# Two-layer trunk (RG-LRU, then forgetting attention): per-head work moved between query groups, output operands made in head 14, the first MLP product's pools swapped, small copies and sums on VectorE

## The chip, the cores and the metric

The kernel runs on one core of a Trainium2 chip. The metric is the device time of one execution in microseconds (us). The kernel before took 2306.42 us, the median of three runs (2304.84 to 2311.81).

## The reference

One sequence of 1024 positions, width 1024, goes through two layers in float32. Each layer adds a mixer and then an MLP to the residual stream.

```python
for layer in range(2):
    h = rms_norm(x, mix_norm[layer])
    x = x + (rglru_mixer(h) if layer == 0 else fox_mixer(h))
    x = x + square(relu(rms_norm(x, mlp_norm[layer]) @ w1[layer])) @ w2[layer]

def fox_mixer(h):                       # 16 heads of 64
    q, k, v, f = split(h @ w_in)        # 1024, 1024, 1024, 16 columns
    q, k = rms_norm(heads(q)), rms_norm(heads(k))
    c = cumsum(log_sigmoid(f + b_f))
    s = q @ k.T / 8 + c[t] - c[s]       # causal
    return (softmax(s) @ v) @ w_out
```

## The kernel before, in words

**Precision.** Every float32 product is made from pieces: an operand is split into a high part, rounded on ScalarE, and a low part, the difference, on VectorE or GpSimd, and three matmuls (high·high, low·high, high·low) are summed in PSUM. So each weight unit of 128x512 costs a load on SP's queue (L114, into one of 4 buffers `raw`), a cast on ScalarE (L118) and a subtraction (L119), 3 in 7 of them on VectorE and the others on GpSimd. The activations stand transposed: 128 features by 1024 positions, in two halves of 512.

**Stages.** The program is one straight line that a scheduler lays out on each engine's queue, and each queue is worked off in order. In time: the input is transposed and normed (to 66 us), the RG-LRU mixer (to 235) and its output projection (`mixer_out`, to 325), layer 0's first MLP product W1 (to 620) and second W2 (to 976), the projections of the forgetting attention begin (to 1040), 16 heads of attention (to about 1528, the last head overlapping the output projection, to 1660), then layer 1's W1 (to 1953) and W2 (to 2315).

**MLP products** (`strassen`, `mlp`). W1 and W2 use seven products of half-size blocks, p1, p2, p6, p5, p7, p3, p4 in this order. p6, p5, p7 and p3 use sums of weight blocks: for p6 three raw blocks are loaded into buffers of the pool `sp` (4 buffers), and VectorE makes the sums s1, s2 and s3 (`total`, L390), of which s2 is cast and split for p6. Before W1, `mixer_out` adds the residual (tile `x`), sums its squares into `rho`, and forms p1's to p4's operands from differences `t` (L367) of halves; `x` and `t` lie in a pool `tp` that is closed as W1 begins, so W1's pools take over its addresses and have to wait for its readers. W1's two pools are opened in line L553, first `s{layer}` (raw blocks and sums), then `h{layer}` (hidden blocks, their differences, copies of banks). The norm's mean over features is a matmul with ones over a split `rho` (L161 t_sh, L162 t_sl, then L216 and L217) that is issued behind p1.

**End of W2 in layer 0** (`fin0`, L748). Each finished block of the residual is scaled and split for the attention (L175, L176), squared (L186) and added to `rho` (`sumsq_add`, L187, on GpSimd), for eight blocks of each half. The forget gate's small weight is loaded, cast and subtracted (`decay`, L985).

**Attention.** A head is worked in four groups g of 256 queries (64 groups in all). While one head is scored, the next is prepared in steps (`prepare`): 0, the projection of the second half and its squares (`head_norm`: L779, L781 into a tile `sq`, L161); 1, the other half's projection and the first half's mean (L216), root and split; 2, the second half's mean and split; 3, a values' projection for a pair of heads; 4, its transposes (L842). In a group, `scores` makes 2 rows of 128 queries (L867, L868, then a masked minimum on VectorE, L871, which gives free the bank, and the exponential on ScalarE, L878), `transpose_rows` transposes them (L892) and splits the bank into pth (ScalarE, L161) and ptl (VectorE, L162), and `weigh_values` multiplies with the values (L908) into the one bank `pv`. At a group's end `put_out` copies that bank to a tile `po` (L915, ScalarE) and stores it (L916); the bank can be written again only then.

After two heads `divide` finishes the pair: reciprocals of the denominators are transposed (L925), copied (L927) and stored (L928), and for each of 4 groups the two partial outputs (L936, L937) and the broadcast reciprocals (L940) are loaded, added and multiplied on VectorE (L944, L945) and stored as `o_sp` (L947). The partial outputs use the same two buffers `sq` as the heads' squares. `load_out` reads `o_sp` back (L956, two buffers `hn`), casts (L958) and subtracts (L959): the operands of the output projection.

The order of all this is the loop at L1083:

```python
for i, (h, g) in enumerate(groups):
    if g < 2 and h > 0: prepare(h + 1, g + 1)
    if g == 2: prepare(h + 1, 3)
    if g == 3: prepare(h + 1, 4); prepare(h + 2, 0)
    if g == 2 and h >= HPT and h % HPT == 0: divide(h // HPT - 1)
    if h == NH - 1 and g == 1: ...      # load_out(0) to load_out(6)
    scores(i + 1)
```

Of the kernel before, what the change touches and what calls it, by code (L numbers as in the profile page):

```python
# [12 lines left out]
ALU = mybir.AluOpType  # L13
# [3 lines left out]
P = 128  # L17
# [6 lines left out]
def tile_trunk(  # L24
# [28 lines left out]
    nc = tc.nc  # L53
# [3 lines left out]
    NH = fox_b_f.shape[1]  # L57
    HD = D // NH
    HPT = P // HD
    KT = D // P  # L60
# [9 lines left out]
    def scope(name, side=None):  # L70
        return tc.tile_pool(name=name, bufs=1, side=side, reuse_waits="tile")
# [23 lines left out]
    rho = const.tile([P, S], F32, name="rho")  # L95
# [81 lines left out]
            xl[:, sl], src, g, xh[:, sl].bitcast(F32), ALU.mult, ALU.subtract  # L177
        )

    def sumsq_add(ssq, src, first, hf, tmp):  # L180
        acc = ssq[:, HALVES[hf]]
        if first:
            nc.scalar.activation(acc, src, AF.Square)
        else:
            sq = tmp("sq")
            nc.scalar.activation(sq, src, AF.Square)  # L186
            nc.gpsimd.tensor_tensor(acc, acc, sq, ALU.add)  # L187

    def rsqrt(dst, v, bias, tmp, table):

# [52 lines left out]
    with scope("start") as st:  # L243
        tmp = temps(st, sq=2)
# [28 lines left out]
        def col(name, k=0):  # L273
            c = cols[name] + k
            return pcol[:, c:c + 1]
# [49 lines left out]
        ssq = st.tile([P, S], F32, name="ssq")  # L325
# [213 lines left out]
    def mlp(layer, units, final, between, tf, first):  # L539
# [10 lines left out]
            for u in range(NP):  # L550
                first2["p1", u] = weight_unit(raw_unit(load_w2(layer, 0)(11, u)))

        with scope(f"s{layer}") as sp, scope(f"h{layer}") as hp:  # L553
            sets[0] = 1

            def norm():
                for hf in range(2):
                    norm_rho(rho, hf, lambda n, dt=F32: hp.tile(
                        [P, H], dt, tag="t", name=f"t_{n}", bufs=6), hf)

            n_groups = FF // (4 * P)

            def group(g):
                held, h = {}, {}

                def store(p, q, t):
                    nc.sync.dma_start(hid[2 * g + q][PRODUCTS.index(p)], t)

                def hidden(key, q, c, hf):
                    t = hp.tile([P, H], F32, tag="h", name="h", bufs=8)  # L570
                    nc.vector.scalar_tensor_tensor(
                        t, c, 0.0, rho[:, HALVES[hf]], ALU.max, ALU.mult
                    )
                    nc.scalar.activation(t, t, AF.Square)
                    h[key, q] = t

                def evict(p, q, ps):
                    if p in ("p1", "p6", "p5"):
                        held[p, q] = t = hp.tile([P, H], F32, tag="cp", name="cp", bufs=6)
                        nc.scalar.copy(t, ps)  # L580
                        return
                    if p == "p4":
                        hidden(21, q, ps, 0)
                    else:
                        t = held[{"p2": "p1", "p7": "p5", "p3": "p6"}[p], q]
                        nc.vector.tensor_tensor(t, ps, t, ALU.add)
                        hidden({"p2": 11, "p7": 22, "p3": 12}[p], q, t, p != "p2")
                    if p == "p4":
                        new = lambda: hp.tile([P, H], F32, tag="t", name="t", bufs=6)
                        for o, src in operand_sums(new, *(h[k, q] for k in (11, 12, 21, 22))):  # L590
                            store(o, q, src)

                def behind():
                    if g == 0:
                        norm()
                    if g == n_groups - 1:
                        ahead_right(sp)

                return SimpleNamespace(
                    load=load_w1(layer, g), right=lambda p, i: units[p][i], evict=evict,  # L600
                    behind=behind,
                    before_last=ahead_left if g == n_groups - 1 else lambda: None,
                )

            strassen(2, [group(g) for g in range(n_groups)], sp, 2, first)
        ops_st.close()
        between()
        with scope(f"t{layer}") as tp, scope(f"x{layer}") as xp, scope(f"q{layer}") as sp2:
# [7 lines left out]
            tmp = temps(xp, sq=3)  # L616
# [31 lines left out]
    with ExitStack() as ys_st:  # L648
        ys = pair_tiles(ys_st.enter_context(scope("ys", "right")), "b")
        with scope("lru") as lp:  # L650

            def tmp(name, dt=F32):
                return lp.tile([P, S], dt, tag=name, name=f"l_{name}", bufs=1 + (name == "g"))
# [30 lines left out]
            for c in range(KT):  # L684
# [9 lines left out]
                g = tmp("g")  # L694
# [47 lines left out]
    acts2, begun = [], set()  # L742
# [5 lines left out]
    def fin0(p, d, hf, xd, tmp):  # L748
        sl = HALVES[hf]
        gain_split(acts2[d], xd, col("mix", KT + d), sl)  # L750
        sumsq_add(rho, xd, hf not in begun, hf, tmp)
        begun.add(hf)
        nc.sync.dma_start(x_sp[d][:, sl], xd)

# [5 lines left out]
    with scope("fox") as fp:  # L760
        tmp = temps(fp, {"rs": "sh", "hf": "sl"}, hn=2, sq=2, sh=2)
# [150 lines left out]

        def put_out(h, g, po):
            o = fp.tile([P, 2 * P], F32, tag="po", name="po", bufs=2)
            nc.scalar.copy(o, po[:, :2 * P])  # L915
            nc.sync.dma_start(  # L916
                v_sp[h // HPT, :, (h % HPT) * HD:(h % HPT + 1) * HD, g * 2 * P:(g + 1) * 2 * P],
                o,
            )
# [33 lines left out]
        def load_out(p):  # L953
            for sl in HALVES:
                o = tmp("hn")
                nc.sync.dma_start(o, o_sp[p][:, sl])  # L956
                hi, lo = (a[:, sl] for a in os_[p])
                nc.scalar.copy(hi, o)  # L958
                nc.gpsimd.tensor_tensor(lo, o, hi.bitcast(F32), ALU.subtract)  # L959
# [14 lines left out]
        def decay():  # L974

            Q = 32
            M = Q + NH
            raw = row("raw")[:, :KT * M].rearrange("p (k m) -> p k m", m=M)
            nc.vector.memset(raw, 0.0)
            nc.sync.dma_start(  # L980
                raw[:, :, :NH], fox_w_in[0][:, 3 * D:].rearrange("(k p) n -> p k n", p=P)
            )
            w = row("wf", F32R)[:, :KT * M].rearrange("p (k m) -> p k m", m=M)
            nc.scalar.copy(w, raw)
            nc.gpsimd.tensor_tensor(  # L985
                w[:, :, Q:M], raw[:, :, :NH], w[:, :, :NH].bitcast(F32), ALU.subtract
            )

            z = row("z")[:NH]
            for hf in (1, 0):  # L990
                sl = HALVES[hf]
                ps = bank("pj")
                for k, a2 in enumerate(acts2):
                    for m in range(2):
                        nc.tensor.matmul(
                            ps[:M], w[:, k, :], a2[m][:, sl],
                            start=k == 0 and m == 0, stop=k == KT - 1 and m == 1,
                        )
                nc.scalar.copy(z[:, sl], ps[Q:M])
                nc.vector.tensor_tensor(z[:, sl], ps[:NH], z[:, sl], ALU.add)  # L1000
            return z
# [22 lines left out]
        def prepare(h, step):  # L1024

            if h >= NH:
                return
            if step == 0:
                heads[h], halves["begin"], halves["end"] = query_key(h)
                if h % HPT == 0:  # L1030
                    dens[h // HPT] = fp.tile([P, HPT * TT], F32, tag="den", name="den", bufs=3)
                if h > 1:
                    decay_rows(h)
            if step == 0:
                halves["begin"](0)
            if step == 1:
                halves["begin"](1, lambda hf: halves["end"](0))
            if step == 2:
                halves["end"](1)
            if step > 2:  # L1040
                p, hf = divmod(h + 1, HPT)
                if p < NH // HPT:
                    if hf == 0 and step == 3:
                        vals[p], halves["v"], halves["v_end"] = values(p)
                    halves["v" if step == 3 else "v_end"](hf)
# [4 lines left out]
        def scores(i):  # L1050
            if i < len(groups):
                h, g = groups[i]
                rows_of[i] = [softmax_rows(h, 2 * g + u) for u in range(2)]
# [28 lines left out]
        scores(0)  # L1082
        for i, (h, g) in enumerate(groups):  # L1083

            if g < 2 and h > 0:
                prepare(h + 1, g + 1)
            if g == 2:
                prepare(h + 1, 3)
            if g == 3:
                prepare(h + 1, 4)  # L1090
                prepare(h + 2, 0)
            if g == 2 and h >= HPT and h % HPT == 0:
                divide(h // HPT - 1)
            if h == NH - 1 and g == 1:
                for p in range(KT - 1):
                    load_out(p)
            scores(i + 1)
            Es = rows_of.pop(i)
            po = bank("pv")
            for b2 in range(g + 1):  # L1100
                pt = transpose_rows(Es, b2, b2 == g)
                finish(waiting)
                waiting = (h, g, b2, po, pt)
# [57 lines left out]
```

## Time and profile before

| | |
|---|---|
| median of three runs | 2306.42 us |
| the profiled execution | 2316.57 us, its span 2314.8 us |
| TensorE busy | 2203.2 us, 95% of the span |
| VectorE busy | 1641.5 us, 71% |
| ScalarE busy | 1221.4 us, 53% |
| GpSimd busy | 654.2 us, 28% |
| mean granted TensorE clock | 0.979 of 2.4 GHz |

An engine's busy time is summed over its instructions. The granted clock is 1 where TensorE runs at 2.4 GHz and 0.5 where it runs at 1.2 GHz; a stretch with 0.8 spent two fifths of its time at the lower level. What bounds the kernel is TensorE, so what can be gained at a given number of matmuls is its idle time (111 us over the span) and the time that it spends at the lower clock.

### The profile page before, as it was taken

To read this page: it belongs to the slowest core of one execution; us is meant where nothing else is said; L and a number is where in the kernel's file an instruction comes from. 1 tells how busy PE (TensorE), PEld (TensorE's weight loads), DVE (VectorE), ACT (ScalarE), POOL (GpSimd) and SP (SyncE) were. 2 spreads that over 40 slices of the span, in tenths; PEclk is the share of its full clock that TensorE was granted. 3 is DMA by queue.
4 is the path that set the end of the run, shared out by engine and by line. 5 is a ranking of instruction groups with operands and counts; after the bars stand their busy time and mean duration, and the time that the engine had idled before them with its cause. 6 is when DMAs were issued, how large, how long until landed. Compare 5 with 4: busy or idle time off the path is not lost.

```text
span 2314.8 us, 30591 instructions
## 1 busy us (share of the span) xinstructions
PE 2203.2 (95%) x10074; PEld 1794.0 (78%) x10074; DVE 1641.5 (71%) x2563; ACT 1221.4 (53%) x2143; POOL 654.2 (28%) x585
## 2 busy tenths in 40 slices
PE   7999989999999999999999999979899999999999
PEld 5888767888778888768777887767778887787887
DVE  7767576767568888868777777764667575788774
ACT  5677564444334444567765766663644444343444
POOL 5333233323223323521111111023333223232221
PEclk9999999999999999999999999999999999999999
DMA  5111345556468655422333233334455564786554
GB/s 201 44 52 37 117 140 189 200 183 207 138 237 272 217 171 185 150 55 60 95 86 86 77 83 84 86 120 155 131 196 198 186 203 146 265 263 204 169 176 124
DMA packets 300165, 346.55 MB, mean 150 GB/s; under 512 B 59718, under 2 KB 190502, under 8 KB 299974
## 3 DMA queue, kind: packets, MB, share of 16 engines
q1 hardware_dynamic: 299760, 344.29, 46.6%
q8 instruction: 79, 1.29, 0.2%
q14 instruction: 80, 0.66, 0.1%
q10 hardware_dynamic: 246, 0.31, 0.1%
HBM read 243.91 MB, written 92.21 MB: 145 GB/s over the span
## 4 chain that ended last, share of the span: by engine, by line
PE 69%; DVE 8%; DMA 7%; issue 6%; POOL 4%; ACT 4%; SPq 1%; ACTq 0%; POOLq 0%; DVEq 0%
PE ps_b L443 16%; PE ps_b L444 16%; PE ps_b L442 15%; PE ps_b L156 5%; PE ps_b L158 5%; PE ps_b L157 5%; PE ps_b L908 2%; POOL whl L119 2%; DMA wraw<-in_mlp_w_dram 2%; PE ps_b L892 2%; DMA t_hn<-o_sp 1%; DVE l_xc L719 1%; PE ps_b L867 1%; PE ps_b L868 1%; DMA r_sp<-rd 1%
## 5 line engine op out<-in xcount | busy, mean ns | idle before, releaser
L119 POOL TENSOR_TENSOR whl<-wraw,whl 128x512 fp32r<-128x512 f32 x231 | 332.8, 1443 | 755.3 <-ACT whl L118 678.4
L118 ACT CAST whl<-wraw 128x512 fp32r<-128x512 f32 x352 | 218.3, 621 | 430.5 <-PE ps_b L444 145.2
L443 PE MATMUL ps_b<-thl,whl 128*128 128x512 f32 x1024 | 402.5, 393 | 7.7 <-POOL whl L119 4.6
L442 PE MATMUL ps_b<-thl,whl 128*128 128x512 f32 x1024 | 400.9, 393 | 7.2 <-ACT thl L118 5.2
L444 PE MATMUL ps_b<-thl,whl 128*128 128x512 f32 x1024 | 401.7, 393 | 0.0
L442 PE MATMUL ps_b<-up,whl 128*128 128x512 f32 x768 | 301.9, 396 | 14.5 <-ACT whl L118 14.5
L443 PE MATMUL ps_b<-up,whl 128*128 128x512 f32 x768 | 304.3, 397 | 7.5 <-POOL whl L119 7.1
L444 PE MATMUL ps_b<-up,whl 128*128 128x512 f32 x768 | 302.2, 394 | 0.0
L119 POOL TENSOR_TENSOR whl<-s,whl 128x512 fp32r<-128x512 f32 x108 | 158.0, 1467 | 403.3 <-ACT whl L118 358.4
L156 PE MATMUL ps_b<-ah,whl 128*128 128x512 f32 x640 | 256.9, 402 | 10.5 <-ACT ah L958 6.9
L158 PE MATMUL ps_b<-al,whl 128*128 128x512 f32 x640 | 255.8, 400 | 4.8 <-DVE al L176 2.8
L157 PE MATMUL ps_b<-ah,whl 128*128 128x512 f32 x640 | 256.4, 401 | 0.0
L443 PEld LDWEIGHTS ps_b<-thl,whl 128*128 128x128 f32 x1024 | 193.8, 189 | 52.1 <-POOL whl L119 7.2
L118 ACT CAST whl<-s 128x512 fp32r<-128x512 f32 x192 | 118.1, 622 | 217.2 <-PE ps_b L444 173.4
L442 PEld LDWEIGHTS ps_b<-thl,whl 128*128 128x128 f32 x1024 | 193.3, 189 | 50.5 <-ACT thl L118 6.1
L119 DVE TENSOR_TENSOR thl<-traw,thl 128x512 fp32r<-128x512 f32 x224 | 208.8, 948 | 27.6 <-ACT thl L118 27.5
L444 PEld LDWEIGHTS ps_b<-thl,whl 128*128 128x128 f32 x1024 | 193.9, 189 | 40.7 <-DVE thl L119 0.7
L442 PEld LDWEIGHTS ps_b<-up,whl 128*128 128x128 f32 x768 | 144.9, 189 | 49.6 <-ACT whl L118 17.7
L443 PEld LDWEIGHTS ps_b<-up,whl 128*128 128x128 f32 x768 | 145.7, 190 | 42.1 <-POOL whl L119 9.2
L444 PEld LDWEIGHTS ps_b<-up,whl 128*128 128x128 f32 x768 | 145.8, 190 | 32.4
L636 DVE TENSOR_TENSOR x<-ps_b,x 128x512 f32<-128x512 f32 x224 | 142.1, 681 | 38.0 <-PE ps_b L444 30.0
L119 DVE TENSOR_TENSOR whl<-wraw,whl 128x512 fp32r<-128x512 f32 x121 | 89.8, 742 | 98.0 <-ACT whl L118 97.9
(215 smaller groups left out, 4173.3 us busy)
## 6 DMA issues: line engine op xcount, KB each, us to landing
wraw<-in_mlp_w_dram SPq DMA_DIRECT2D x448, 256.0 KB
traw<-hid SPq DMA_DIRECT2D x224, 256.0 KB
hid<-t SPq DMA_DIRECT2D x128, 256.0 KB
hid<-h SPq DMA_DIRECT2D x96, 256.0 KB
x<-x_sp SPq DMA_DIRECT2D x64, 256.0 KB
x_sp<-x SPq DMA_DIRECT2D x48, 256.0 KB
wraw<-in_lru_w_in_dram SPq DMA_DIRECT2D x32, 256.0 KB
wraw<-in_fox_w_in_dram SPq DMA_DIRECT2D x64, 128.0 KB
```

What stands on the lines that cost most here:

```text
L118: nc.scalar.copy(hl[:, 0], src)
L119: (sub or nc.vector).tensor_tensor(hl[:, 1], src, hl[:, 0].bitcast(F32), ALU.subtract)
L156: nc.tensor.matmul(ps, wh, xh, start=k == 0, stop=False)
L157: nc.tensor.matmul(ps, wl, xh, start=False, stop=False)
L158: nc.tensor.matmul(ps, wh, xl, start=False, stop=k == KT - 1)
L442: nc.tensor.matmul(ps, wh, xh, start=fresh and i == 0, stop=False, **go)
L443: nc.tensor.matmul(ps, wl, xh, start=False, stop=False, **go)
L444: nc.tensor.matmul(ps, wh, xl, start=False, stop=i == NP - 1, **go)
L636: nc.vector.tensor_tensor(xd, ps, xd, ALU.add)
L719: nc.vector.scalar_tensor_tensor(xc, xp[:, j:j + S], col("cw", j * KT + c), xc, ALU.mult, ALU.add)
L892: nc.tensor.transpose(pt[:, n * P:(n + 1) * P], Es[u][:, b * P:(b + 1) * P], ident)
L908: nc.tensor.matmul(po[:, :2 * P], vb, src[:, n].rearrange("p u q -> p (u q)"), start=first and n == 0 and m == 0, stop=last and n == 1 and ...
```

## The change

It has five parts. The two pools of W1 are opened in the other order. `put_out` copies on VectorE. The sums of squares of product p4's blocks, and the forget weight's low part, are made on VectorE. In the attention loop the steps of `prepare` are spread differently: step 3 from group 2 to group 1, step 2 from group 1 to group 2, step 4 from group 3 to group 2, and `divide` from group 2 to group 1. `load_out` runs in head 14 (groups 1 and 2) for the first six pairs, and in head 15's group 0 for the seventh.

```diff
-    def sumsq_add(ssq, src, first, hf, tmp):
+    def sumsq_add(ssq, src, first, hf, tmp, eng=None):
...
-            nc.gpsimd.tensor_tensor(acc, acc, sq, ALU.add)
+            (eng or nc.gpsimd).tensor_tensor(acc, acc, sq, ALU.add)
...
-        with scope(f"s{layer}") as sp, scope(f"h{layer}") as hp:
+        with scope(f"h{layer}") as hp, scope(f"s{layer}") as sp:
...
-        sumsq_add(rho, xd, hf not in begun, hf, tmp)
+        sumsq_add(rho, xd, hf not in begun, hf, tmp, nc.vector if p == "p4" else None)
...
-            nc.scalar.copy(o, po[:, :2 * P])
+            nc.vector.tensor_copy(o, po[:, :2 * P])
...
-            nc.gpsimd.tensor_tensor(
+            nc.vector.tensor_tensor(
                 w[:, :, Q:M], raw[:, :, :NH], w[:, :, :NH].bitcast(F32), ALU.subtract
             )
...
-            if g < 2 and h > 0:
-                prepare(h + 1, g + 1)
+            if g == 0 and h > 0:
+                prepare(h + 1, 1)
+            if g == 1:
+                prepare(h + 1, 3)
             if g == 2:
-                prepare(h + 1, 3)
+                if h > 0:
+                    prepare(h + 1, 2)
+                prepare(h + 1, 4)
             if g == 3:
-                prepare(h + 1, 4)
                 prepare(h + 2, 0)
-            if g == 2 and h >= HPT and h % HPT == 0:
+            if g == 1 and h >= HPT and h % HPT == 0:
                 divide(h // HPT - 1)
-            if h == NH - 1 and g == 1:
-                for p in range(KT - 1):
+            if h == NH - 2 and g in (1, 2):
+                for p in range(3 * g - 3, 3 * g):
                     load_out(p)
+            if h == NH - 1 and g == 0:
+                load_out(KT - 2)
```

What the scheduler makes of it is seen in the queues. The first place is SP's queue at the start of layer 0's W1: L114 loads weights, L509 stores the residual and L567 stores hidden blocks.

```order
 L114 DMA wraw<-in_mlp_w_dram 128x2x256
 L509 DMA x_sp<-x 128x512 x2
-L114 DMA wraw<-in_mlp_w_dram 128x2x256 x2
+L114 DMA wraw<-in_mlp_w_dram 128x2x256 x3
 L509 DMA x_sp<-x 128x512 x2
-L114 DMA wraw<-in_mlp_w_dram 128x2x256 x5
+L114 DMA wraw<-in_mlp_w_dram 128x2x256 x11
 L567 DMA hid_449<-h 128x512
```

Eleven weight loads now stand together ahead of the first hidden block's store, where there were five, and one more stands ahead of the last residual stores.

The second place is VectorE's queue at the same start: `t` and `up` are the differences of halves and their low parts, s_2749 and s_2751 are s1 and s2 for p6, and t_rs belongs to the norm.

```order
+L390 TENSOR_TENSOR s_2749<-wraw 128x512
 L367 TENSOR_TENSOR t<-x,t 128x512
-L119 TENSOR_TENSOR up_2648<-x,up_2648 128x512
 L367 TENSOR_TENSOR t<-x 128x512
+L119 TENSOR_TENSOR up_2666<-x,up_2666 128x512
 L119 TENSOR_TENSOR up_2658<-t,up_2658 128x512
-L119 TENSOR_TENSOR up_2666<-x,up_2666 128x512
 L119 TENSOR_TENSOR up_2663<-t,up_2663 128x512
 L367 TENSOR_TENSOR t<-x,t 128x512
-L197 SCALAR_TENSOR_TENSOR t_rs<-ps_b_2715,eps,t_rs 128x512
+L390 TENSOR_TENSOR s_2751<-s_2749,wraw 128x512
```

The sums for p6 moved ahead of the norm's operations and between the last differences of `mixer_out`; the norm's own matmuls L216 and L217 moved on TensorE from behind p1 to between p6's matmuls.

The third place is a pair's `divide` in the attention, on SP's queue (the second pair of heads).

```order
 L936 DMA t_sq<-v_sp 128x256
 L937 DMA t_sq<-v_sp 128x256
-L916 DMA v_sp<-po 2x64x256
 L928 DMA r_sp<-rd 16x128
+L940 DMA r<-r_sp 64x256 x4
+L916 DMA v_sp<-po 2x64x256
+L968 DMA q_9719<-c_sp 4x1024
+L947 DMA o_sp<-t_sq 128x256
+L940 DMA r<-r_sp 64x256 x2
```

The loads of the reciprocals now stand directly behind their store, with the next store of `po` behind them. On TensorE 119 rows of the queue stand between a pair's L925 and the L216 that first needs a buffer from that `divide`, where there were 93. On VectorE the copies of `put_out` stand between the minima of the scores and behind products of `divide`:

```order
L871 ISA E,mx<-ps_b_10475,zero 128x512
L871 ISA mx 128x1
L945 TENSOR_TENSOR t_sq<-t_sq,r 128x256
L871 ISA E,mx<-ps_b_10480,mask,mx 128x512
L871 ISA mx 128x1
L915 COPY po<-ps_b_10403 128x256
L197 SCALAR_TENSOR_TENSOR t_rs<-ps_b_10434,eps,t_rs 128x512
L198 TENSOR_SCALAR t_rs<-t_rs 128x512
```

These are rows of the changed kernel alone; the copy of the bank `ps_b_10403` stood on ScalarE's queue before.

## Rows read from the trace of the kernel before

**Rows 1.** The page's busy times: busy us, share of the span, instructions.

```profile
PE 2203.2 (95%) x10074; PEld 1794.0 (78%) x10074; DVE 1641.5 (71%) x2563; ACT 1221.4 (53%) x2143; POOL 654.2 (28%) x585
```

**Rows 2.** Windows: length, busy us of each engine, granted clock, DMA share, GB/s.

```profile
335.00:360.00 25.00, 15.42 (x55) 11.37 (x54) 19.79 (x31) 12.68 (x21) 7.57 (x4) 0.80 0.49 157
960.00:1000.00 40.00, 31.49 (x111) 21.29 (x110) 26.08 (x29) 21.74 (x36) 23.82 (x21) 0.83 0.40 111
1040.00:1500.00 460.00, 439.19 (x2422) 368.91 (x2422) 348.20 (x787) 313.58 (x666) 67.11 (x144) 0.98 0.31 82
1500.00:1600.00 100.00, 81.88 (x403) 65.01 (x402) 50.33 (x118) 48.82 (x105) 23.63 (x34) 0.91 0.37 115
1660.00:1700.00 40.00, 31.25 (x123) 23.40 (x122) 27.26 (x41) 22.78 (x38) 11.43 (x8) 0.91 0.47 149
```

**Rows 3.** Waits of TensorE, 325 to 360 us: total us, times, longest us.

```profile
PE ps_b L442 <- ACT whl L118: 5.1, 1, 5.1
PE ps_b L443 <- POOL whl L119: 2.7, 1, 2.7
PE ps_b L216 <- ACT t_sh L161: 1.0, 1, 1.0
```

**Rows 4.** Waits of SP's queue, 324 to 340 us, and its timeline (start us, us).

```profile
SPq L114 <- DVE t L367: 6.6, 2, 5.9
...
327.15 9.70 SPq L114 DMA_DIRECT2D wraw<-in_mlp_w_dram  x5
```

**Rows 5.** Timeline of VectorE, ScalarE and GpSimd, 343 to 349 us.

```profile
343.66 0.69 DVE L390 TENSOR_TENSOR s<-s,wraw 128x512 f32<-128x512 f32 x1
...
344.38 0.62 ACT L118 CAST whl<-s 128x512 fp32r<-128x512 f32 x1 [1.83 <-DVE s L390]
...
345.08 3.40 POOL L119 TENSOR_TENSOR whl<-s,whl 128x512 fp32r<-128x512 f32 x1 [14.76 <-ACT whl L118]
```

**Rows 6.** Waits of TensorE, 960 to 1000 us.

```profile
PE ps_b L443 <- POOL whl L119: 3.3, 1, 3.3
PE ps_b L995 <- POOL wf L985: 3.1, 1, 3.1
```

**Rows 7.** Timeline of GpSimd, 960 to 990 us.

```profile
977.32 6.82 POOL L187 TENSOR_TENSOR rho<-rho,t_sq 128x512 f32<-128x512 f32 x4
```

**Rows 8.** Waits of TensorE in the attention, 1040 to 1500 us.

```profile
PE ps_b L216 <- ACT t_sh L161: 15.3, 6, 2.9
PE ps_b L908 <- ACT po L915: 2.3, 6, 0.4
```

**Rows 9.** Chain of waits through one `divide`, 1107 to 1132 us: start us, us, what.

```profile
1110.49 4.56 DMA r_sp<-rd
...
1125.87 4.63 DMA o_sp<-t_sq
...
1130.57 0.64 ACT t_sq L781
```

**Rows 10.** Timeline of TensorE: a pair's L925, and the L216 behind its `divide`.

```profile
1109.01 0.27 PE L925 MATMUL ps_b<-ident,rc 128*16 128x128 f32 x1
...
1131.90 0.50 PE L216 MATMUL ps_b<-t_sh,ones_h 128*128 128x512 f32 x1 [2.10 <-ACT t_sh L161]
```

**Rows 11.** Waits of VectorE, 1100 to 1500 us.

```profile
DVE t_sq L944 <- DMA t_sq<-v_sp: 12.3, 11, 2.3
DVE t_sq L945 <- DMA r<-r_sp: 11.9, 6, 2.2
```

**Rows 12.** Groups of instructions by form, 1040 to 1600 us: xcount | busy, mean ns | idle before.

```profile
L915 ACT COPY po<-ps_b 128x256 f32<-128x256 f32 x64 | 23.9, 373 | 3.2 <-DMA v_sp<-po 2.4 <-PE ps_b L908 0.8
```

**Rows 13.** The same view, VectorE from 1040 to 1500 us.

```profile
L162 DVE TENSOR_TENSOR v<-ps_b,v 128x256 fp32r<-128x256 f32 x26 | 10.9, 420 | 3.5 <-ACT v L161 3.0
```

**Rows 14.** Waits of TensorE at the attention's end, 1500 to 1600 us.

```profile
PE ps_b L156 <- ACT ah L958: 6.9, 5, 2.1
PE ps_b L908 <- ACT po L915: 4.3, 2, 2.2
```

## The prediction

> **What bounds the kernel now.** I read the page first: TensorE is busy for 2203.2 of 2314.8 us, 95% of the span, and VectorE for 71% [rows 1]. The change removes no matmul (the queues hold as many before and after), so it can win only TensorE's idle time and the time at the lower of its two clock levels, 1.2 instead of 2.4 GHz. Then I cut the span into stretches, to see where either occurs and the change touches it [rows 2]. There are five places. At the start of layer 0's W1 TensorE is idle for 25.00 - 15.42 = 9.6 us, at a granted clock of 0.80 (two fifths of the time at 1.2 GHz). At the start of layer 1's W1 it is 40.00 - 31.25 = 8.8 us at 0.91. Where the attention's projections begin it is 8.5 us at 0.83. In the attention proper it is 20.8 us of 460 at 0.98, and at its end 18.1 us of 100 at 0.91. Then I asked in each stretch which wait ended last: the waits of TensorE, the queue of the engine that it waited for, and so back.
>
> **W1's start, the swapped pools.** TensorE waits 5.1 us for p6's cast weights, 2.7 for their low part and 1.0 for the norm's split [rows 3]. The cast came at 344.38, right behind the sum s2 of 343.66, and the low part took GpSimd 3.40 us from 345.08 [rows 5]. The sum was late because its raw blocks were: SP's queue waited 6.6 us for VectorE's last differences `t`, so its five loads dragged over 9.70 us from 327.15 on [rows 4]. Those buffers lie where `mixer_out`'s temporaries lay; nothing in the data asks for that wait. With the pools swapped the sum buffers lie over earlier tiles, and by the order p6's sums stand among the last differences, whose end is the last thing that SP waited for, about 327.15 + 9.70 = 336.9. One sum (0.69) and one cast (0.62) later is 338.2, and the low part is there by about 340, where p6's first matmuls came at about 345 and 348.5. Idle time falls from 9.6 to some 2.5 us: **-7**. The clock lost at most 25 x 0.4 / 2 = 5 us, less what of it fell into idle time; I take **-3** of it. Bounds of the two: -4 (the low part and the norm still late, the clock as it was) to -13. The hidden blocks take over the addresses of the temporaries instead; they are first written behind p2, when the temporaries are done, so I cost that at nothing. The first hidden stores now queue behind eleven loads; what reads them is W2, hundreds of microseconds later.
>
> Layer 1 shows the same picture: 8.8 us of idle time, at a clock that cost at most 40 x 0.18 / 2 = 3.6 us [rows 2]. I take **-6** and **-2**; bounds -3 to -12.
>
> **Start of the attention's projections.** Of the 8.5 us, 3.3 wait for a weight's low part and 3.1 for the forget weight's [rows 6]. The first comes before p4 and stays. The second is made on VectorE now, and GpSimd loses the four sums that held it for 6.82 us [rows 7], which VectorE makes in some 4 x 0.69. But the forget weight's load waits for a fill on VectorE itself, behind these four sums. So I take **-2**; bounds +3 (the four sums on the path of the norm) to -7 (both waits and the clock).
>
> **The attention, `divide` one group earlier.** Once per pair of heads TensorE waits for the split of a head's squares, 15.3 us in six waits [rows 8]. The chain of waits says why: the reciprocals' store takes 4.56 us to land, loads and products follow, the third store of the result takes 4.63 us, and only then may ScalarE write the squares into that buffer, at 1130.57 [rows 9]. From the pair's L925 at 1109.01 that is 21.6 us, and TensorE was there 2.10 us too early [rows 10]. Its own work between the two took 22.9 - 2.1 = 20.8 us for 93 rows of its queue, 0.22 us each; now 119 rows lie between, about 26.6 us, against the 21.6 plus about 1.3 for square and split. The stall goes, with 3.7 us to spare. What is late next is VectorE, which waits for `divide`'s loads for 12.3 + 11.9 us [rows 11]; I leave 0.5 us per pair for it: -15.3 + 3 = **-12**. The low clock in this stretch cost up to 460 x 0.04 / 2 = 9 us; **-4** if half of it followed the stalls.
>
> **`put_out` on VectorE.** ScalarE's copy took 373 ns, 64 of them 23.9 us [rows 12]. VectorE needs about 420 ns for 128x256 out of PSUM [rows 13]: 64 x 0.42 = 27 us more for an engine busy for 348.2 of 460 us, so 76% becomes 81%. Since the next product waits for this bank, the bounds are -6.6 (TensorE's waits for the copy, 2.3 here and 4.3 at the end [rows 8, 14], go) and +27 (each copy on the path). I take **+4**: the nearest row is the same wait now, 0.4 us at a time, and by the order other work of TensorE now stands between most copies and the next product.
>
> The Trainium skill, on the page "VectorE: DVE Perf Modes", section Specifications, states that VectorE sits closer to SBUF and ScalarE closer to PSUM, which speaks against this move. The trace agrees in direction, 420 against 373 ns [rows 12, 13]; by the rule the sum would be 64 x 0.05 = 3 us worse if every copy were waited for, by the rows it is in the +4 already.
>
> **Output operands during head 14.** At the attention's end TensorE waits 6.9 us for casts of loaded pairs, and 4.3 for copies that stand behind such casts on ScalarE [rows 14]. The casts now come a little earlier in the queues, and the copies no longer stand behind them. Against that, head 15 has no next head to prepare, so TensorE there follows VectorE, which gets 4 or 5 more copies (2 us) and the last products of two pairs. By the order the first load still waits for a buffer of head 15's own projections. I take **-5** of the 18.1 us; bounds +4 to -18.
>
> **Sum.** -10 - 8 - 2 - 12 - 4 + 4 - 5 = -37 us. The profiled execution took 2316.57 us and would take about 2280; it stood 10.2 us above the median of the three runs (2306.42), so I set the difference against the median: **2269 us**.
>
> **The rivals.**
>
> *VectorE takes back the attention.* For it: 81% busy, in order, with waits of up to 2.3 us for DMA [rows 11] ahead of copies that free the one bank `pv`. Against it: such waits stand there now and leave TensorE only 2.3 us short on that bank's copy. If the copies eat the attention's -12 - 4 and the end's -5, only W1's and the projections' -20 remain: 2286, with 2278 to 2298 around it.
>
> *Slower than before.* The same mechanism in full: a copy stands behind each of VectorE's waits for `divide`'s loads, and each is passed on to TensorE. That is (12.3 + 11.9) / 6 = 4.0 us per pair, plus eight copies of 0.42, so 7.4 us per pair and 52 us for seven. Against the other terms (-41 without the +4) this gives +11, 2317. It decides from 41 / 7 = 5.9 us per pair on. Against it: the DMA waits of VectorE stand in the trace now, and TensorE loses 0.4 us at a time to that bank while they do [rows 8].
>
> *The swap does not free the loads.* SP's queue might still be held by a weight buffer, since the loads behind p6's go through four of them. Then W1's 18 us stay, and the time is 2287.
>
> *More is won.* If every stall named here and the lost clock go, the bounds -13, -12, -7, -19 and -10 (about half of the end's) make -61, some 2245; half way, 2255.
>
> **How the numbers follow.** A measurement of this kernel can tell about 0.3%, 7 us, from no change. I give the forecast (2260 to 2280) 0.55, more 0.13, VectorE taking the attention back 0.18, the swap without effect 0.08, slower 0.06. The range 2248 to 2296 holds the first, most of the second and third, and the fourth: it leaves out about 2 in 10. All but the slower case end under 2299.5, but a mixture of the third and fourth would not: faster 0.88, same 0.06, slower 0.06.
>
> **What would show each step.** Right: in both W1 starts no wait of TensorE over 1.5 us for p6's weights, SP's loads no longer waiting for `t`, and a granted clock of 0.95 or more; in the attention no wait for the heads' split squares, waits for the copy of `pv` under 0.6 us each and about 5 us in all; GpSimd's sums behind p4 gone. Wrong: p6's weights still late by 3 us or more; waits of TensorE on VectorE (ptl, mx, po) of more than 2 us per pair; the squares' wait still there at half or more, which would mean that the chain of `divide` itself grew; the end of the attention as long as before, which would mean that VectorE bounds it.

## The result and the profile after

The changed kernel took 2268.35 us (median of 4 runs, 2263.93 to 2276.55), the kernel before 2307.53 beside it. The ratio of the runs is 0.9828 (that of the two medians alone 0.9830), with a 95% interval of 0.9802 to 0.9854, so 39.7 us less (34 to 46). 2269 was forecast. The profiled execution took 2263.93 us, below its median, and that of before 2316.57, above; the two profiles differ by 52.6 us, so what their stretches differ by is more than the 39.7, and the sizes of the parts are taken from the runs.

The page's busy times, to be read against [rows 1]:

```profile
PE 2182.3 (96%) x10074; PEld 1781.0 (79%) x10074; DVE 1661.3 (73%) x2632; ACT 1195.5 (53%) x2079; POOL 647.3 (29%) x580
```

The matmuls are the same in number. VectorE is busy for 20 us more, ScalarE for 26 us less. The stretches that answer to [rows 2] (length, busy us of PE, PEld, DVE, ACT and POOL, granted clock, DMA share, GB/s); each begins 0 to 45 us earlier than it did:

```profile
335.00:360.00 25.00, 22.80 (x88) 17.33 (x89) 22.19 (x31) 15.59 (x27) 9.71 (x6) 0.93 0.41 133
946.00:986.00 40.00, 30.96 (x111) 20.95 (x110) 25.27 (x34) 21.43 (x35) 17.89 (x16) 0.83 0.42 114
1026.00:1466.00 440.00, 433.11 (x2467) 367.22 (x2466) 369.10 (x854) 298.81 (x622) 67.44 (x148) 1.00 0.32 86
1466.00:1540.00 74.00, 58.66 (x289) 45.07 (x288) 44.43 (x104) 38.42 (x78) 21.36 (x29) 0.88 0.42 122
1615.00:1655.00 40.00, 36.43 (x148) 28.33 (x147) 32.37 (x45) 24.64 (x42) 14.31 (x9) 0.96 0.51 159
```

TensorE's idle time went from 9.6 to 2.2 us at layer 0's W1 and from 8.8 to 3.6 at layer 1's. At the start of the attention's projections it stayed (9.0 against 8.5, the clock at 0.83 in both). In the attention it went from 20.8 to 6.9 us, in 440 us that now hold 2467 matmuls where 460 held 2422, and the granted clock from 0.98 to 1.00. At the end 15.3 us of idle time and a clock of 0.88 are left.

Waits of TensorE at layer 0's W1, 325 to 360 us (total us, times, longest), for [rows 3]:

```profile
PE ps_b L443 <- POOL whl L119: 1.8, 1, 1.8
PE ps_b L442 <- ACT cp L580: 1.8, 1, 1.8
```

Waits of SP's queue there, 318 to 340 us, for [rows 4]:

```profile
SPq L114 <- DVE s L390: 8.9, 4, 4.4
SPq L114 <- POOL whl L119: 5.1, 1, 5.1
```

No load waits for `t` any more; the queue waits for buffers of the sums themselves, ahead of need. Of p6's weights only the low part is still late, by 1.8 us, and the copies of p1's banks on ScalarE now end a wait.

In the attention (1026 to 1460 us) the waits of TensorE that answer to [rows 8]:

```profile
PE ps_b L867 <- DVE mx L871: 5.1, 6, 1.1
PE ps_b L217 <- DVE t_sl L162: 1.1, 2, 0.6
PE ps_b L908 <- DVE ptl L162: 0.6, 1, 0.6
```

Neither the squares' split nor a copy of the bank is among them. VectorE's largest waits for a DMA there (from 12.3 us in [rows 11]; L945's 11.9 is gone from the view):

```profile
DVE t_sq L944 <- DMA t_sq<-v_sp: 7.6, 8, 2.0
```

### The profile page after: what moved, and what is told of

Read it like the earlier page. It is cut to its first block, busy times and chain, and to the rows that moved or that the text cites. A ratio compares the mean times of both kernels' runs of the same rounds, so it can differ in the third digit from the quotient of the medians.

```text
span 2262.1 us, 30597 instructions
## 1 busy us (share of the span) xinstructions
PE 2182.3 (96%) x10074; PEld 1781.0 (79%) x10074; DVE 1661.3 (73%) x2632; ACT 1195.5 (53%) x2079; POOL 647.3 (29%) x580
## 4 chain that ended last, share of the span: by engine, by line
PE 68%; DVE 5%; DMA 5%; ACT 3%; issue 2%; POOL 1%; SPq 0%; DVEq 0%; ACTq 0%; POOLq 0%
PE ps_b L443 16%; PE ps_b L444 16%; PE ps_b L442 16%; PE ps_b L158 4%; PE ps_b L157 4%; PE ps_b L156 4%; PE ps_b L908 2%; DMA wraw<-in_mlp_w_dram 2%; PE ps_b L892 2%; PE ps_b L867 1%; PE ps_b L868 1%; POOL whl L119 1%; DMA o_sp<-t_sq 1%; DMA t_hn<-o_sp 1%; DMA t_sq<-v_sp 1%
```

## The experiments

Differences in us are against the kernel before, which ran beside each (the ratio of the runs, less 1, times 2309), unless said otherwise; a difference from the changed kernel is the difference of two such ratios. Every kernel ran in at least four runs.

| kernel | ratio to before (interval) | us |
|---|---|---|
| the change | 0.9828 (0.9802 to 0.9854) | -39.7 |
| before + swapped pools | 0.9938 (0.9924 to 0.9951) | -14 |
| before + order of prepare and divide | 0.9972 (0.9958 to 0.9985) | -6.5 |
| before + copies on VectorE | 1.0015 (1.0001 to 1.0029) | +3.5 |
| before + order + copies | 0.9897 (0.9878 to 0.9916) | -24 |
| change, divide back in group 2 | 0.9973 (0.9963 to 0.9984) | -6 |
| change, prepare's steps back | 0.9862 (0.9847 to 0.9877) | -32 |
| change, copies back on ScalarE | 0.9880 (0.9858 to 0.9902) | -28 |
| change, load_out back in head 15 | 0.9867 (0.9845 to 0.9888) | -31 |
| change, sums back on GpSimd | 0.9839 (0.9814 to 0.9863) | -37 |
| change + more work on ScalarE | 0.9881 (0.9860 to 0.9901) | -27 |
| copies back + more work on VectorE | 1.0058 (1.0043 to 1.0073) | +13 |
| change + p3's sums on VectorE | 0.9811 (0.9794 to 0.9828) | -44 |

**The swap alone.** On the kernel before:

```diff
-        with scope(f"s{layer}") as sp, scope(f"h{layer}") as hp:
+        with scope(f"h{layer}") as hp, scope(f"s{layer}") as sp:
```

> The kernel before with W1's two pools opened in the other order, nothing else. Theory A (stage by stage reading of the two traces): each start of W1 loses 5 to 6 us less, so 10 to 12 us less than before in all (about 2296). Rival B (the prediction's size): 18 us less (about 2289). In the trace both expect no wait of the p6 loads for the differences t; A expects waits of about 1.8 us each for p6's low part and for the copies of banks to stay.

It gave 14 us (11 to 18), between the two sizes. The waits at layer 0's W1 (325 to 365 us) show what it leaves:

```profile
PE ps_b L443 <- POOL whl L119: 1.8, 1, 1.8
PE ps_b L442 <- ACT cp L580: 1.3, 1, 1.3
```

The clock is 1.00 from 335 to 360 us there, 0.93 in the changed kernel. It is 0.80 in the four kernels of this case without the swap, 0.93 in eight with it and 1.00 in two; what parts the last two values no run shows.

**The order alone.** The kernel before with the new places of `prepare`'s steps 2, 3 and 4 and of `divide`; the loop's two hunks of the diff, without the one on `load_out`.

> The kernel before with the steps of prepare and divide at the groups of the change, while put_out stays on ScalarE, load_out in head 15 and the pools as before. Theory A (the stall for the heads' squares and the low clock behind it were the attention's loss): 18 to 24 us less than before, no wait for the squares' split left, granted clock 1.00 from 1040 to about 1470. Rival B (ScalarE, relieved of the copies, made the gain): 8 us less or under, with waits for the copy of the bank in its place.

Only 6.5 us (3.5 to 9.7), so theory A's size fell. The time is of rival B's size, but its sign is missing, since no wait for a copy took the stall's place. The waits of TensorE from 1032 to 1490 us:

```profile
PE ps_b L867 <- DVE mx L871: 9.9, 8, 1.7
PE ps_b L908 <- ACT pth L161: 1.7, 3, 0.8
```

The squares' wait went, as A said, and VectorE took it over: TensorE waits up to 1.7 us for the minimum that frees the scores' bank. The clock is 0.99 there, not 1.00.

**The copies alone.** On the kernel before:

```diff
-            nc.scalar.copy(o, po[:, :2 * P])
+            nc.vector.tensor_copy(o, po[:, :2 * P])
```

> The kernel before with put_out's copy on VectorE, nothing else. Theory A: 0 to 6 us less than before (the waits for ScalarE's copy, 2.3 and 4.3 us, go; the six waits for the squares stay at 15 us). Rival B (ScalarE's relief is the gain): 12 us less or more. Rival C (VectorE becomes the bound): slower by 4 us or more.

Slower by 3.5 us (0.2 to 6.7). That is C's direction, just under its size; A and B both forecast a gain. The waits of TensorE from 1032 to 1500 us, and of VectorE:

```profile
PE ps_b L867 <- DVE mx L871: 21.9, 12, 2.4
PE ps_b L216 <- ACT t_sh L161: 4.0, 6, 1.3
```

```profile
DVE t_sq L944 <- DMA t_sq<-v_sp: 32.6, 18, 3.2
```

With `divide` in its old place VectorE waits 32.6 us for the loads of partial outputs, where it waited 12.3 (and 3.0 for the reciprocals, where it waited 11.9) [rows 11], and the minima queue behind:

```profile
1176.74 0.42 DVE L944 TENSOR_TENSOR t_sq<-t_sq 128x256 f32<-128x256 f32 x1 [2.63 <-DMA t_sq<-v_sp]
...
1177.74 0.61 DVE L871 CUSTOM_DVE_ANT_0 E<-ps_b,mask,mx 128x384 f32<-128x384 f32 x1
```

That the squares' wait shrinks from 15.3 to 4.0 us fits a TensorE that arrives later; this was not tested apart.

**The change with divide back in group 2.** On the changed kernel:

```diff
-            if g == 1 and h >= HPT and h % HPT == 0:
+            if g == 2 and h >= HPT and h % HPT == 0:
```

> The changed kernel with divide put back to group 2, all else as changed. Theory A (the place of divide decides the stall): 12 to 22 us more than the changed kernel, with six waits of 1 to 3 us for the squares' split and a clock below 1.00 in the attention. Rival D (the moved head means and values' transposes alone do it): within 5 us of the changed kernel and no such wait.

33 us above the changed kernel: A's mechanism, more than its size, and D falls. The waits of TensorE from 1024 to 1490 us:

```profile
PE ps_b L216 <- ACT t_sh L161: 23.9, 6, 4.7
```

The stall is 4 us per pair where it was 2.5 in the kernel before, and the clock 0.97.

**Order and copies together, and the copies taken back.** First the two parts that gave -6.5 and +3.5 alone, together on the kernel before.

> The kernel before with two parts of the change together: the order of prepare and divide, and put_out's copy on VectorE. Alone they gave -6.5 and +3.5 us. If they only add (theory Sum), about 3 us less than before. If they need each other (theory Pair: without the new order the copies stand behind divide's loads on VectorE, without the copies VectorE reaches divide's fourth product before its load has landed), 18 to 26 us less, with no waits of TensorE for the squares, at most 6 us of waits for the scores' minima, and a granted clock of 1.00 up to about 1480 us.

24 us less (19 to 28): they need each other. Beside the order alone, the copies are worth 17 us. The waits of TensorE (1026 to 1480 us) are those of the changed kernel, and the clock is 1.00:

```profile
PE ps_b L867 <- DVE mx L871: 5.4, 6, 1.1
PE ps_b L217 <- DVE t_sl L162: 0.8, 3, 0.3
```

Then the changed kernel with `nc.scalar.copy` again in `put_out`.

> The changed kernel with put_out's copy back on ScalarE. Theory Pair: 15 to 22 us more than the changed kernel, VectorE's waits for divide's loads of partial outputs at 15 us or more (7.6 in the changed kernel), waits of TensorE for the minima about 10 us. Theory Sum: within 4 us of the changed kernel.

12 us above the changed kernel, a little under what Pair expected, and outside Sum's 4. VectorE's waits for partial outputs are back at 16.1 us, and a second thing shows in the groups of VectorE's instructions by form (1030 to 1480 us; count, busy us, mean ns, idle before):

```profile
L162 DVE TENSOR_TENSOR t_sl<-t_sq,t_sh 128x512 fp32r<-128x512 f32 x27 | 25.7, 952 | 7.6 <-ACT t_sh L161 7.1
L818 DVE TENSOR_TENSOR k<-t_hn,k 64x512 fp32r<-64x512 f32 x28 | 24.1, 862 | 0.9
L788 DVE SCALAR_TENSOR_TENSOR t_hn<-t_hn,gqk,t_hf 128x512 f32<-128x512 f32 x28 | 20.8, 743 | 0.0
```

In the changed kernel (1020 to 1475 us) the same forms read:

```profile
L788 DVE SCALAR_TENSOR_TENSOR t_hn<-t_hn,gqk,t_hf 128x512 f32<-128x512 f32 x28 | 25.6, 913 | 0.0
L162 DVE TENSOR_TENSOR t_sl<-t_sq,t_sh 128x512 fp32r<-128x512 f32 x28 | 19.3, 690 | 3.5 <-ACT t_sh L161 3.1
L818 DVE TENSOR_TENSOR k<-t_hn,k 64x512 fp32r<-64x512 f32 x28 | 19.2, 687 | 0.8
```

With the copy on ScalarE two kinds of VectorE's operations take longer, with it on VectorE one. In the kernel before none of the three does (688, 687 and 748 ns, 1040 to 1470 us), so this comes with the new order. The timelines say which operations they are. In the kernel with the order alone (GpSimd, VectorE, then ScalarE, around 1200 us):

```profile
1200.02 1.81 POOL L119 TENSOR_TENSOR vw<-wraw,vw 128x512 fp32r<-128x512 f32 x1 [3.83 <-ACT vw L118]
1202.69 1.44 POOL L119 TENSOR_TENSOR vw<-wraw,vw 128x512 fp32r<-128x512 f32 x1 [0.86 <-ACT vw L118]
```

```profile
1199.92 0.74 DVE L788 SCALAR_TENSOR_TENSOR t_hn<-t_hn,gqk,t_hf 128x512 f32<-128x512 f32 x1
1200.70 1.67 DVE L162 TENSOR_TENSOR t_sl<-t_sq,t_sh 128x512 fp32r<-128x512 f32 x1
...
1203.00 1.67 DVE L818 TENSOR_TENSOR k<-t_hn,k 64x512 fp32r<-64x512 f32 x1
```

```profile
1199.05 0.37 ACT L915 COPY po<-ps_b 128x256 f32<-128x256 f32 x1
1199.32 0.63 ACT L118 CAST vw<-wraw 128x512 fp32r<-128x512 f32 x1
```

The two operations of VectorE that begin while GpSimd subtracts a values' weight take 1.67 us, not 0.69, just ahead of the minima that TensorE waits for. L788, which begins 0.10 us ahead of the first subtraction, keeps its 0.74 us. An operation with one input in PSUM keeps its time as well: L837, at 1188.67 in the changed kernel, begins inside a subtraction and takes 0.69 us. In the changed kernel no copy stands ahead of the cast on ScalarE, and the first subtraction begins 0.13 us ahead of L788 (ScalarE, GpSimd, VectorE):

```profile
1184.01 0.62 ACT L118 CAST vw<-wraw 128x512 fp32r<-128x512 f32 x1
1184.71 1.29 POOL L119 TENSOR_TENSOR vw<-wraw,vw 128x512 fp32r<-128x512 f32 x1 [3.60 <-ACT vw L118]
1184.84 1.71 DVE L788 SCALAR_TENSOR_TENSOR t_hn<-t_hn,gqk,t_hf 128x512 f32<-128x512 f32 x1
```

So L788 alone is held up; the second subtraction, at 1188.57, takes 1.28 us and slows none of these forms. The kernel with the copy back shows the picture of the order alone in five pairs of heads, and there TensorE's wait for the minimum is 1.7 us each time, where it is 0.8 to 1.1 in the changed kernel. These waits are 9.6 us in place of 5.1 in all, 4.5 of the 12 us; how the rest comes about was not taken apart.

**Is it ScalarE's relief?** The change with the tile copied onto itself on ScalarE, and the opposite: the copy back on ScalarE, and the tile copied onto itself on VectorE.

```diff
             nc.vector.tensor_copy(o, po[:, :2 * P])
+            nc.scalar.copy(o, o)
```

```diff
             nc.scalar.copy(o, po[:, :2 * P])
+            nc.vector.tensor_copy(o, o)
```

> The changed kernel, whose tile po is copied onto itself on ScalarE behind VectorE's copy: 64 more operations of 128x256 on ScalarE, so that it has as much to do as before, while TensorE's bank is still freed by VectorE. Theory Relief (the gain of the moved copy is ScalarE's relief): about 12 us more than the changed kernel, as with the copy back on ScalarE. Theory Lag (the gain is where VectorE's operations come to stand against divide's loads and GpSimd's subtractions): within 4 us of the changed kernel, with VectorE's waits for partial outputs near 8 us.

> The copy back on ScalarE, and the tile copied onto itself on VectorE behind it: 64 more operations on VectorE than with the copy back, the bank freed by ScalarE. Theory Lag: near the changed kernel (within 6 us), since VectorE's queue is laid out as if it had the copies; theory Relief: as with the copy back on ScalarE (12 us or more above the changed kernel).

The first is 12 us above the changed kernel, as much as taking the copy back cost: Relief's size. Lag's expectation of the time falls, though its mark is there, since VectorE waits only 5.1 us for partial outputs. What came back is the meeting with GpSimd and the wait for the minima (VectorE's groups, and waits of TensorE, 1025 to 1475 us):

```profile
L162 DVE TENSOR_TENSOR t_sl<-t_sq,t_sh 128x512 fp32r<-128x512 f32 x27 | 24.6, 910 | 14.5 <-ACT t_sh L161 14.1
L818 DVE TENSOR_TENSOR k<-t_hn,k 64x512 fp32r<-64x512 f32 x27 | 23.5, 869 | 0.8
```

```profile
PE ps_b L867 <- DVE mx L871: 9.7, 6, 1.8
```

So the moved copy pays through ScalarE's queue and not through the bank. Here too the copy onto itself stands directly ahead of the cast of a values' weight (1191.63 and 1191.94 us, for one pair), and the same two operations are held up: it is the place of the copy as much as the load on the engine. Two reservations stay. The added operation also makes ScalarE wait for VectorE's copy. And each of these edits makes the scheduler lay out the queues anew: against the changed kernel, the copies left out, about 40 of VectorE's 2568 operations stand in another order here, about 110 with the copy back and about 210 in the second kernel. Neither was tried apart.

The second kernel, 53 us above the changed one, is far outside Lag's 6 us; it lies in Relief's open range, but 41 us above the copy back that Relief takes as its measure, so it decides little between them. There VectorE waits 32.0 us for partial outputs, and TensorE 14.5 us for VectorE's ptl.

**prepare's steps back in their groups**, `divide` staying in group 1, on the changed kernel.

> The changed kernel with prepare's steps back in their old groups, divide staying in group 1. If divide's place alone carried the gain in the attention: within 4 us of the changed kernel. If the steps are needed too, as the title of the change has it: 8 us or more above it, with waits for the squares' split or for the minima in the attention.

8 us above the changed kernel (the intervals overlap a little, 0.9847 to 0.9877 against 0.9802 to 0.9854): most likely the steps are needed too, but `divide`'s place carries more. No wait for the squares' split is left; TensorE waits for the splits of the transposed rows instead (1025 to 1475 us):

```profile
PE ps_b L892 <- DVE ptl L162: 4.7, 7, 2.0
PE ps_b L867 <- DVE mx L871: 3.7, 5, 0.7
PE ps_b L842 <- DVE t_sq L837: 3.0, 4, 1.1
```

**load_out back in head 15's group 1**, on the changed kernel.

> The changed kernel with load_out back in head 15's group 1. The prediction's step: the changed kernel's end of the attention would be 5 us longer, so about 5 us more. Rival (the casts are held by their two buffers and not by the place in the program): within 3 us of the changed kernel.

9 us above the changed kernel; the intervals overlap by a little (0.9845 to 0.9888, against 0.9802 to 0.9854). The waits of TensorE at the end (1480 to 1570 us):

```profile
PE ps_b L156 <- ACT ah L958: 8.2, 5, 4.5
PE ps_b L908 <- ACT pth L161: 2.4, 2, 1.9
```

In the changed kernel (1475 to 1560 us):

```profile
PE ps_b L908 <- DVE ptl L162: 5.3, 2, 4.3
PE ps_b L156 <- ACT ah L958: 4.5, 6, 1.0
```

The casts are late by 1.0 us at most, where one was 4.5 us late; but one split on VectorE now takes 4.3 us off TensorE.

**The sums.** The changed kernel with p4's sums and the forget weight's low part back on GpSimd, and the changed kernel with p3's sums on VectorE as well:

```diff
-        sumsq_add(rho, xd, hf not in begun, hf, tmp, nc.vector if p == "p4" else None)
+        sumsq_add(rho, xd, hf not in begun, hf, tmp, nc.vector if p in ("p3", "p4") else None)
```

> The changed kernel with p4's sums of squares and the forget weight's low part back on GpSimd. The prediction's step: 2 us more. From the two traces, where this stretch is as long with as without: within 2 us of the changed kernel.

> A candidate: the changed kernel with product p3's sums of squares on VectorE too. In the changed kernel they hold GpSimd for 6.7 us ahead of three weights' low parts, and TensorE waits 3.2 us for the first of them. If that wait goes: 3 to 6 us less than the changed kernel. If VectorE only takes the delay over: within 2 us.

Taking them back costs 2.5 us by the ratios, moving more gains 4; both intervals overlap with the changed kernel's, so neither is settled. The stretch itself says why so little happens. In the changed kernel (946 to 986 us) the wait for the forget weight only changed its name, and TensorE waits 2.8 us for the norm's split:

```profile
PE ps_b L443 <- POOL whl L119: 3.2, 1, 3.2
PE ps_b L995 <- DVE wf L985: 2.8, 1, 2.8
PE ps_b L216 <- ACT t_sh L161: 2.8, 1, 2.8
```

The last wait is not the price of the move, since it is 4.0 us with the sums back on GpSimd. With p3's sums on VectorE too, the first goes and the norm pays (940 to 990 us):

```profile
PE ps_b L216 <- ACT t_sh L161: 6.8, 1, 6.8
PE ps_b L995 <- DVE wf L985: 2.8, 1, 2.8
```

That kernel has the lowest median of all, 2264.95 us; against the changed kernel it is not faster beyond doubt.

## Why the prediction was right, and where its steps were not

**W1, -18.** Right in mechanism: the loads' wait for `t` is gone, and p6's sums come among the last differences. Over-sized by 4 us: the swap alone gave 14. Of the waits it named, the low part stayed at 1.8 and 1.6 us, above the 1.5 us set as the mark, with GpSimd at it for 2.75 us beside a busy VectorE (1.32 us for its next one), and the wait for p1's bank copies (1.8 and 1.5 us) was not foreseen. The clock reached 0.93 and 0.96, where 0.95 was the mark.

**The projections' start, -2.** Not settled by the runs, and small either way. The text said that the forget weight's load stands behind VectorE's own work; that is what the trace shows.

**The attention, "-15.3 + 3 = -12", "-4" and "+4".** Together -12 was forecast and -24 measured for order and copies. The stall went as worked out, and the clock came back whole. The step that failed is the copy's "+4". Its nearest row, the wait for the copy of the bank, was the wrong row: the price did not lie in the bank. Alone the copy costs 3.5 us; that this is near the +4 is luck, since another wait made it, that for the minima behind VectorE's waits for `divide`'s loads. In the new order it is worth 12 to 17, in part because the copy no longer delays the cast behind it on ScalarE. The step before it, that the order by itself gives 12 to 16 us, fell too: alone it gave 6.5. The text left 3 us for what is late next, VectorE with its waits for `divide`'s loads. VectorE it was, with 9.9 us of TensorE's waits for the minima; but directly ahead of the longest of these stand the operations that GpSimd's subtractions hold up, which the text did not have.

**The end, -5.** About 9 us, with intervals that overlap a little: of the size that was said, and rather above it. It does not add to the rest, since the swap (14) and order with copies (24) make 38 of the 39.7 us already.

**The sum.** That -37 came so near to -39.7 is in part luck: W1 was 4 us too good, the attention 12 us too poor, and the parts do not add (14, 24, 9 and 2.5 make 50). Half way between 2269 and the 2245 of "More is won" is 2257 and not 2255, which changes nothing. Of the rivals, VectorE taking the attention back is what the copies alone and the order alone each show in part, in TensorE's waits for the minima (21.9 and 9.9 us); with both these are 5.4. The copy's own 46 ns more (419 ns on VectorE in the changed kernel, 373 in [rows 12]) do not decide it. The rule on the engines' places that the prediction weighed there (the Trainium skill, page "VectorE: DVE Perf Modes", section Specifications) bears on these nanoseconds alone, and the trace agrees with its direction.

## What to carry to other kernels

A pool that is opened over another pool's addresses inherits its readers: before a stage's start, look whose wait its first loads end, and let the buffers needed first lie over the tiles that die first. Two moves of which one gains little alone and the other loses can gain together (6.5 less and 3.5 more here, 24 less for both); so take a change's parts out of the whole as well as testing them alone. And price an operation moved off an engine by what stands behind it in that engine's queue, not by its own length.

## What the runs showed that was not expected

A ScalarE busy for about two thirds of the attention is still worth relieving: 64 copies of 373 ns, 24 us of work that no wait of TensorE pointed to beyond 6.6 us, were worth 12 us in the new order and cost 3.5 in the old one. VectorE's operations on two tiles in SBUF took 1.67 in place of 0.69 us when they began while GpSimd's subtraction ran; a shift of the subtraction by 0.23 us against VectorE's queue, less than one copy takes on ScalarE, went with one such operation more and with waits of TensorE of 1.7 in place of 0.8 to 1.1 us in five pairs of heads. And TensorE's granted clock, 0.98 with a stall of 2 to 3 us once per pair, was 1.00 through 440 us whose waits were 1.1 us at most; with the copies alone, whose waits reached 2.4 us, it was 0.99.
